# First mixer of a decoder trunk: values of eight heads projected at once as [token, feature], masks and key stacks made by transfers, one pool for weights and values

## The chip, the cores and the metric

The kernel runs on one core of one Trainium2 chip. The metric is the device time of one execution in microseconds (us), as the median of three runs. TensorE is written PE (its weight load PEld), VectorE DVE, ScalarE ACT, GpSimd POOL and SyncE SP. SP here only starts transfers; POOL starts some too.

## The reference, cut to what matters

The computation is a trunk of two layers over 512 positions of 1024 features, in float32. The stage that the change touches is the first mixer, "hybrid", which has eight dilated heads (A) and eight sparse heads (B):

```python
def hybrid_ab_mixer(u, table, w_in, cq_g, wq_b, wq_idx, w_out):
    proj = u @ w_in
    qa, ka, va, cq, kb, vb, k_idx, w_idx = jnp.split(proj, _offsets(EVEN_SIZES), axis=-1)
    o_a = dilated_mixture(qa, ka, va, table[:, :A_HEADS])
    cq = rmsnorm(cq, cq_g)
    qb = cq @ wq_b
    q_idx = cq @ wq_idx
    o_b = dsa_attention(qb, kb, vb, q_idx, k_idx, w_idx, table[:, A_HEADS:], topk)   # topk = 128
    return jnp.concatenate([o_a, o_b], axis=-1) @ w_out

def one_block(...):                      # of dsa_attention, 128 queries at a time
    sc = relu(q_idx . k_idx)             # 8 index heads of 32 features
    score = sum over heads of sc * w_idx
    idx = top_k(where(s <= t, score, -inf), 128)
    logits = q . k[idx] * dh**-0.5 + bias[dist]
    o = softmax(logits) @ v[idx]
```

Around it the first layer has a SwiGLU feed-forward block before and one behind, each added by half; the second layer is the same with a sliding-window mixer in the middle.

## The kernel before, in words

All 512 positions lie in the chip's memory as eight tiles of 128 features x 512 tokens. Every float32 operand is kept as a high and a low part, and a product is three matmuls (L389, L390 and L391 in `chunk`, the helper of the projections; L869 to L871 in `out_proj`). A program, `Plan.emit`, writes down the order of every engine's instructions before the kernel is built: each operation has a cost and a due time, each pool of tiles a number of slots (`CAPACITY`: 58 half tiles "s2", 8 banks "ps", 20 weight tiles "d4", 2 value tiles "v"). The engines then run these orders as written; an instruction that waits holds up all behind it on its engine. The same is true of the transfers started by SP and by POOL.

The stages follow one another: feed-forward, hybrid, feed-forward, feed-forward, sliding, feed-forward. Each stage starts with a norm, whose sums over features are matmuls with a column of ones (L452).

In the hybrid stage `project(j)` makes, for one pair of heads j, three things. Values: a projection as [feature, token], scaled on DVE (`v_turned`, L740), transposed by four PE matmuls with the identity (L744), and split into high and low by ACT (L755) and DVE (L325, the helper of all subtractions). Keys: `k_stack` scales on DVE (L717), and each of two heads gets a tile of 128 partitions that holds its 64 features twice, the high part by ACT (L399) and a copy on ACT (L725) or POOL (L728), the low part by two subtractions (L325) of 64 x 512 on DVE or POOL. Queries: `q_stack` (L701, L399, L325), the subtraction on DVE or POOL. A pair of A heads takes its query weights from `hyb_in`, a pair of B heads from `wq_b`.

`select` makes the masks of the B heads. PE computes the index scores (L964), ACT the relu (L967), DVE the weighted sum (L971 to L978). For the query blocks 1, 2 and 3 DVE then runs sixteen rounds of "eight largest" (L986) and "replace them" (L988), and closes each block (L994) with a bf16 mask that is zero where a key was taken and very negative elsewhere. These steps are strung through the order of DVE between the work of the A heads.

`head` has, for each of four query blocks of 128, 256, 384 and 512 keys: score matmuls (L780, L781), in a B head a further matmul that adds the mask to the bank (L783: the bf16 identity times the mask), a DVE step that adds the position bias and takes the row bound (L787), the exponential on ACT (L796). Then reciprocal (L806), the normalisation on POOL (L813) or ACT (L817), transposes (L829), the split by ACT (L831) and DVE (L325), the product with the values (L845, L846), and the output in ACT (L850) and DVE (L851). `out_proj` follows for all heads in two parts. The bias of a head is one transfer of 256 KB out of a table (`toeplitz`, L693, SP).

A weight tile that "lands" is loaded by SP (L338), split on ACT (L356, L357), and its low part is finished by a transfer started by POOL (L359) that adds the original to the negated high part. In the hybrid stage most weights come like this.

## Time and profile before

| | us |
|---|---|
| three runs | 1829.66, 1831.09, 1831.96 |
| median | 1831.09 |
| the profiled execution, whole | 1832.38 |
| its span on the core | 1830.6 |
| PE busy in the span | 1807.2 |

The profiled execution lies 1.29 us above the median, and 1.78 us of it lie outside the span. The granted clock of PE was 0.995 of full speed over the span. The page gives for each engine the time in which it was executing. The stage views give the same for a stretch. The timelines list single instructions with their start and duration; matmuls overlap their successors, so that the distance between two starts, not the duration, is what one of them takes.

### The profile page before, as it was taken

What the parts mean: (1) busy time and instruction counts of PE and PEld (TensorE: products, weight loads), DVE (VectorE), ACT (ScalarE), POOL (GpSimd) and SP (SyncE); (2) the same over time, 40 slices, a digit from 0 to 9 for tenths busy, and PEclk for the clock granted to TensorE, in tenths of its full rate; (3) what the DMA queues carried; (4) which work ended last, traced back from release to release, by engine and by line L of the source; (5) the groups of instructions that cost most, each with busy time, mean ns of one, the idle gap of its engine ahead of it and who ended that gap; (6) DMA issues with size and microseconds to landing.
All of it is one profiled execution on the core that took longest, in us unless ns stands there. A gap on an engine that the chain in (4) does not pass through costs nothing.

```text
span 1830.6 us, 28269 instructions
## 1 busy us (share of the span) xinstructions
PE 1807.2 (99%) x11036; PEld 1612.7 (88%) x11036; DVE 1319.3 (72%) x2225; ACT 969.2 (53%) x1600; POOL 170.5 (9%) x228
## 2 busy tenths in 40 slices
PE   9999999999999999999999999999999999999997
PEld 6889989888878889998998989989788889899896
DVE  8575857559977897586588866848468798577483
ACT  6343625658768555253355534625679755255263
POOL 2100000115524000000000000000124200000000
PEclk9999999999999999999999999999999999999999
DMA  6713423785745314232343224313844523243231
GB/s 215 245 58 114 122 64 113 198 209 119 162 112 138 103 48 126 92 105 81 109 117 97 83 91 127 118 56 105 229 95 102 150 70 116 70 127 116 70 104 46
DMA packets 75141, 211.55 MB, mean 116 GB/s; under 512 B 12976, under 2 KB 17168, under 8 KB 75008
## 3 DMA queue, kind: packets, MB, share of 16 engines
q1 hardware_dynamic: 58176, 176.88, 30.6%
q0 software_dynamic: 16688, 32.85, 9.8%
q8 instruction: 86, 1.41, 0.3%
q14 instruction: 47, 0.39, 0.1%
q10 hardware_dynamic: 144, 0.03, 0.0%
HBM read 205.92 MB, written 8.47 MB: 117 GB/s over the span
## 4 chain that ended last, share of the span: by engine, by line
PE 89%; DVE 4%; ACT 3%; DMA 2%; issue 1%; POOL 0%; SPq 0%; DVEq 0%; ACTq 0%; POOLq 0%
PE ps L389 14%; PE ps L390 14%; PE ps L391 14%; PE ps L613 12%; PE ps L615 12%; PE ps L614 12%; DVE d L325 1%; PE ps L869 1%; PE ps L870 1%; PE ps L871 1%; PE ps L829 1%; ACT s L796 1%; DMA d<-in_w 1%; PE ps L1155 1%; PE ps L1157 1%
## 5 line engine op out<-in xcount | busy, mean ns | idle before, releaser
L325 DVE TENSOR_TENSOR d<-d,d 128x1024 fp32r<-128x1024 f32 (+3 forms) x415 | 448.8, 1096 | 186.6 <-ACT d L346 138.3
L346 ACT CAST d<-d 128x1024 fp32r<-128x1024 f32 (+3 forms) x415 | 388.0, 949 | 328.6 <-DMA d<-in_w 209.0
L613 PE MATMUL ps<-s,d 128*128 128x256 f32 x1904 | 539.5, 283 | 0.0
L615 PE MATMUL ps<-s,d 128*128 128x256 f32 x1904 | 538.8, 283 | 0.0
L614 PE MATMUL ps<-s,d 128*128 128x256 f32 x1904 | 538.8, 283 | 0.0
L389 PE MATMUL ps<-s,d 128*128 128x512 f32 (+1 forms) x1252 | 496.0, 396 | 2.2 <-DVE d L325 2.0
L390 PE MATMUL ps<-s,d 128*128 128x512 f32 (+1 forms) x1252 | 489.8, 391 | 0.4 <-DVE s L411 0.3
L391 PE MATMUL ps<-s,d 128*128 128x512 f32 (+1 forms) x1252 | 489.2, 391 | 0.0
L613 PEld LDWEIGHTS ps<-s,d 128*128 128x128 f32 x1904 | 365.4, 192 | 0.5
L614 PEld LDWEIGHTS ps<-s,d 128*128 128x128 f32 x1904 | 365.4, 192 | 0.4
L615 PEld LDWEIGHTS ps<-s,d 128*128 128x128 f32 x1904 | 365.4, 192 | 0.0
L391 PEld LDWEIGHTS ps<-s,d 128*128 128x128 f32 (+1 forms) x1252 | 235.8, 188 | 50.2
L389 PEld LDWEIGHTS ps<-s,d 128*128 128x128 f32 (+1 forms) x1252 | 236.2, 189 | 49.7 <-DVE d L325 2.9
L390 PEld LDWEIGHTS ps<-s,d 128*128 128x128 f32 (+1 forms) x1252 | 236.2, 189 | 46.9 <-DVE s L411 1.2
L626 ACT COPY d<-ps 128x512 f32<-128x512 f32 x136 | 79.8, 587 | 250.0 <-PE ps L615 249.7
L685 DVE SCALAR_TENSOR_TENSOR s<-ps,s 128x512 f32<-128x512 f32 x88 | 60.7, 690 | 140.9 <-PE ps L391 140.9
L325 DVE TENSOR_TENSOR s<-s,s 128x512 fp32r<-128x512 f32 (+2 forms) x190 | 126.4, 675 | 8.8 <-ACT s L399 6.4
L565 DVE TENSOR_TENSOR d<-d 128x512 f32<-128x512 f32 x136 | 91.6, 688 | 2.3
L565 DVE TENSOR_TENSOR d<-d,d 128x512 f32<-128x512 f32 x136 | 90.2, 687 | 1.5
L629 DVE TENSOR_TENSOR d<-ps,d 128x512 f32<-128x512 f32 x102 | 70.1, 687 | 16.8 <-PE ps L615 16.1
L359 POOL DMA_DIRECT2D d<-in_swa_in x10 | 8.7, 865 | 731.6 <-DMA d<-in_swa_in 693.2
L356 ACT CAST d<-d 128x1024 fp32r<-128x1024 f32 (+3 forms) x69 | 55.0, 807 | 32.6 <-DMA d<-in_swa_in 13.4
(152 smaller groups left out, 1929.9 us busy)
## 6 DMA issues: line engine op xcount, KB each, us to landing
d<-in_w SPq DMA_DIRECT2D x238, 512.0 KB, 3.7
d<-in_w SPq DMA_DIRECT2D x32, 384.0 KB, 3.1
d<-in_hyb_in SPq DMA_DIRECT2D x22, 512.0 KB, 5.5
d<-in_hyb_in POOLq DMA_DIRECT2D x22, 512.0 KB, 6.7
d<-in_swa_in SPq DMA_DIRECT2D x10, 512.0 KB, 5.5
d<-in_swa_in POOLq DMA_DIRECT2D x10, 512.0 KB, 7.6
tab<-rv POOLq DMA_DIRECT2D x4, 1024.0 KB, 20.0
s<-tab SPq DMA_DIRECT2D x16, 256.0 KB, 5.5
```

Source lines behind the costliest of these rows:

```text
L325: return lambda: eng.tensor_sub(out(), a(), b().bitcast(F32))
L346: alts = [("act", ns[0](n), lambda: nc.scalar.copy(hl.at(0, o), raw.t[:, c]))]
L389: nc.tensor.matmul(o, wl, xh.t, start=i == 0, stop=False)
L390: nc.tensor.matmul(o, wh, xl.t, start=False, stop=False)
L391: nc.tensor.matmul(o, wh, xh.t, start=False, stop=i == n - 1)
L565: return lambda: eng.tensor_add(o.t[:, oc], a.t[:, ac], o.t[:, oc])
L613: nc.tensor.matmul(o, wl, xh, start=start and m == 0 and k == 0, stop=False, skip_group_check=True)
L614: nc.tensor.matmul(o, wh, xl, start=False, stop=False, skip_group_check=True)
L615: nc.tensor.matmul(o, wh, xh, start=False, stop=k == 3, skip_group_check=True)
L626: self.act(act_ns(S, False), lambda: nc.scalar.copy(view(q, c), bank(ps)), [ps], [(q, key)])
L629: self.dve(vec_ns(S), lambda: nc.vector.tensor_add(view(q, c), bank(ps), view(q, c)), [ps, (q, key)], [(q, key)])
L685: self.dve(dve_ns(S), lambda ps=ps, x=x: nc.vector.scalar_tensor_tensor(x.t, ps.t, 0.5, x.t, op0=OP.mult, op1=OP.add), [ps, x], [x])
```

## The change

Only the hybrid stage is rewritten; the sliding stage shares `k_stack`, `v_split` and `head`.

- Values. `values()` is called for j = 0 and j = 4, for four pairs of heads each. The x tiles are now the stationary side, 128 tokens wide, and 512 columns of weights (all eight heads) the moving side; the product lies in four banks "mv" as [token, feature], as the product with the probabilities needs it. There is no scaling by a tile of row factors (L740) and no transpose (L744) in this stage: the row factor is one number per partition, applied by the ACT copy (high part) and a DVE step (low part). The number of matmuls is the same.
- Masks. The mask matmul and the bf16 identity go. For each B head `masked()` starts four transfers of its bias by SP, of 128, 256, 384 and 512 keys, and three by POOL that add the mask of the blocks 1, 2 and 3 to it in place, from the score tile itself, which now holds the mask in float32.
- Key stacks. One ACT copy and one DVE subtraction make the high and low part of both heads in a tile of 128 x 1024, and four transfers by SP, of 64 partitions and 256 KB, copy them into the two stacks.
- Pools. Value tiles and key tiles take slots of the weight pool, which has 22 now.

The diff, cut to its core:

```diff
-CAPACITY = {"s2": SLOTS, "ps": 8, "d4": 20, "v": 2}
+CAPACITY = {"s2": SLOTS, "ps": 8, "d4": 22}
...
+    def masked(self, tab, h, masks):
+        nc = self.nc
+        b, c = Buf("d4", "toepb", (128, 1024)), self.s2("toepc")
+        out = [(c, 384), (c, 0), (b, 512), (b, 0)]
+        for qb, (buf, at) in enumerate(out):
+            n = (qb + 1) * 128
+            key = (buf, at)
+            self.dma(lambda buf=buf, at=at, n=n: nc.sync.dma_start(buf.t[:, at:at + n], tab[h][:, S - n:]),
+                     [("tab", S, h // 4)], [key], n * 512, self.vt - MASKED)
+            if masks[qb] is not None:
+                self.dma(lambda buf=buf, at=at, n=n, m=masks[qb]: nc.gpsimd.dma_start(
+                    buf.t[:, at:at + n], m.t[:, :n], accum_op=OP.add), [masks[qb], key], [key], n * 512,
+                    self.vt - MASKED + 2000, "pool")
+        return out
...
-    def k_stack(self, ps, rows, pool=True):
+    def k_stack(self, ps, rows):
+        f, both = self.s2("tmp"), Buf("d4", "kt", (128, 1024), F32R)
+        self.dve(vec_ns(S), lambda: nc.vector.tensor_mul(f.t, ps.t, rows.t), [ps, rows], [f])
+        hi, lo = Half(both, 0), Half(both, 1)
+        self.hi(hi, f)
+        self.sub(lambda: lo.t, lambda: f.t, lambda: hi.t, [f, hi], [lo], S, ns=vec_ns)
         k = []
         for h in range(2):
-            kh, kl = self.pair("k")
-            self.hi(kh, f, own, (kh, 0))
...
-            for i, out in enumerate((own, oth)):
-                self.sub(lambda kl=kl, out=out: kl.t[out], lambda own=own: f.t[own],
-                         lambda kh=kh, own=own: kh.t[own], [f, (kh, 0)], [(kl, i)], S, pool)
+            for i in range(2):
+                self.dma(lambda b=b, i=i, h=h: nc.sync.dma_start(
+                    b.t[i * 64:i * 64 + 64].bitcast(F32), both.t[h * 64:h * 64 + 64].bitcast(F32)),
+                    [hi, lo], [(kh, i), (kl, i)], 262144)
...
+    def values(self, src, ops, rs):
+        ps = [self.bank("mv") for _ in range(4)]
+        for u in range(4):
+            w = self.unit(src[:, u * 1024:u * 1024 + 1024], 1024, lands=True)
+            for tb in range(4):
+                def f(u=u, tb=tb, w=w):
...
+                        nc.tensor.matmul(ps[tb].t, xh.t[:, c], wl, start=u == 0 and i == 0, stop=False)
+                        nc.tensor.matmul(ps[tb].t, xl.t[:, c], wh, start=False, stop=False)
+                        nc.tensor.matmul(ps[tb].t, xh.t[:, c], wh, start=False, stop=u == 3 and i == 1)
...
+        for tb in range(4):
+            v = Buf("d4", "v", (128, 8, 2, 64), F32R)
+            self.act(sca_ns(S, 1), lambda v=v, src_=src_, r=r: nc.scalar.activation(
+                v.t[:, :, 0], src_(), AF.Copy, scale=r()), [ps[tb], rs], [(v, 0)])
+            self.dve(vec_ns(S) + 50, lambda v=v, src_=src_, r=r: nc.vector.scalar_tensor_tensor(
+                v.t[:, :, 1], src_(), r(), v.t[:, :, 0].bitcast(F32), op0=OP.mult, op1=OP.subtract),
...
-                if m is not None:
-                    nc.tensor.matmul(ps.t[:, :n], self.identb, m.t[:, :n], start=False, stop=True)
...
-            ps = proj(8 + j if j < 4 else 14 + j, pool=pool)
-            V[j] = self.v_split(self.v_turned(ps, R))
-            K[j] = self.k_stack(proj(4 + j if j < 4 else 10 + j, pool=pool), R, pool or True)
+            if j % 4 == 0:
+                V[j] = self.values(t["hyb_v"][j // 4], ops, rs)
+            V[j] = V[j - j % 4]
+            K[j] = self.k_stack(proj(4 + j if j < 4 else 10 + j, pool=pool), R)
             if j < 4:
-                Q[j] = self.q_stack(proj(j, pool=pool), R, pool or True)
+                Q[j] = self.q_stack(proj(j, pool=pool), R)
...
-                masks[qb] = Buf("s2", "mask", (128, S), BF16)
+                masks[qb] = sc
```

What this moves in the order of the engines is shown at two places.

On PE, at the start of the stage, behind the norm's column sums. A row is line, operation, output bank, stationary and moving tile, and shape; d and s are weight and half tiles. Before, the first index score (L964) stands behind the first value projection:

```order
L389 MATMUL ps<-s_3454,d_3339 128x512
L390 MATMUL ps<-s_3464,d_3337 128x512
L391 MATMUL ps<-s_3454,d_3337 128x512
L932 MATMUL ps<-ident,s_3607 128x104 x4
L964 MATMUL ps<-s_3612,s_3626 128x256
L389 MATMUL ps<-s_3224,d_3371 128x512
```

Now, at the end of the first `values()` call:

```order
L784 MATMUL ps<-d_3463,s_3468 128x512
L785 MATMUL ps<-d_3456,s_3479 128x512
L786 MATMUL ps<-d_3456,s_3468 128x512
L1009 MATMUL ps<-s_3620,s_3632 128x256
L1009 MATMUL ps<-s_3620,s_3643 128x256
L389 MATMUL ps<-s_3244,d_3520 128x512
```

All 96 matmuls of `values()` stand ahead of the first index score (L1009 now), where 24 of the first value projection stood.

On DVE, where the last and longest mask is closed (L994 before, L1039 now), with what each instruction waits for in brackets; `m` holds the eight largest, s_3991 (now s_4035) is the score tile of query block 3. Before, the next head's step (L787) reads a bank that PE has added the mask to:

```order
L988 MATCH_REPLACE s_3991<-m_5233,s_3991 128x512 [waits DVE_49]
L994 TENSOR_SCALAR s_5242<-s_3991 128x512 [waits DVE_49]
L740 TENSOR_TENSOR s_5257<-ps,s_3539 128x512 [waits PE_49,Pool_49]
L787 ISA s_5275,stat<-ps,s_4366 128x512 [waits PE_49,Pool_49]
L787 ISA stat 128x1
```

Now the head's step (L830) reads the bias tile d_601 and waits for the transfer that adds the mask to it (DMASW7, started by POOL):

```order
L1039 TENSOR_SCALAR s_4035<-s_4035 128x512 [waits DVE_49]
L717 SCALAR_TENSOR_TENSOR s_5343<-ps,s_3705 128x512 [waits PE_49]
L325 TENSOR_TENSOR d_5341<-s_5334,d_5341 128x512 [waits DMASW6_49,Activation_49]
L325 TENSOR_TENSOR s_5350<-s_5343,s_5350 64x512 [waits Activation_49]
L325 TENSOR_TENSOR s_5356<-s_5343,s_5356 64x512 [waits Activation_49]
L733 TENSOR_TENSOR s_5390<-ps,s_3546 128x512 [waits PE_49]
L717 SCALAR_TENSOR_TENSOR s_5403<-ps,s_3705 128x512 [waits PE_49]
L830 ISA s_5408,stat<-ps,d_601 128x512 [waits DMASW7_49]
```

Six DVE instructions stand between the close and the wait; PE's next score bank comes free only behind that step.

## Rows read from the trace of the kernel before

**Rows 1.** The page, busy time, share of the span and instructions of each engine.
```profile
PE 1807.2 (99%) x11036; PEld 1612.7 (88%) x11036; DVE 1319.3 (72%) x2225; ACT 969.2 (53%) x1600; POOL 170.5 (9%) x228
```

**Rows 2.** Busy time by stretch: PE, PEld, DVE, ACT, POOL, clock, DMA share, GB/s.
```profile
440.00:500.00 60.00, 60.00 (x317) 50.81 (x317) 58.33 (x176) 47.30 (x107) 36.40 (x45) 1.00 0.67 150
500.00:560.00 60.00, 55.50 (x290) 44.39 (x290) 45.96 (x102) 40.37 (x90) 23.30 (x31) 1.00 0.54 113
367.00:640.00 273.00, 266.59 (x1360) 219.43 (x1359) 224.54 (x550) 195.16 (x399) 94.03 (x113) 1.00 0.58 140
```

**Rows 3.** Line L452 in the hybrid stage: durations, first and last start.
```profile
L452 PE MATMUL ps<-ones,s x24: 164/250/271, 367.1 to 630.5; 128*128 128x1 f32 x24
```

**Rows 4.** PE's waits, 367 to 640 us: waited for, total, times, longest.
```profile
PE ps L845 <- DVE d L325: 1.9, 4, 0.8
PE ps L829 <- ACT s L817: 1.4, 1, 1.4
```

**Rows 5.** PE timeline, block 3 of the first B head: start, duration, instruction.
```profile
522.83 0.39 PE L781 MATMUL ps<-d,s 128*128 128x512 f32 x1
523.06 0.39 PE L783 MATMUL ps<-s,identb 128*128 128x512 bf16 x1
...
523.46 0.45 PE L389 MATMUL ps<-s,d 128*128 128x512 f32 x1
```

**Rows 6.** PE timeline at one group of value transposes.
```profile
416.89 0.60 PE L744 MATMUL ps<-ident,s 128*128 128x128 f32 x4
417.25 0.48 PE L389 MATMUL ps<-s,d 128*128 128x512 f32 x1
417.56 0.39 PE L390 MATMUL ps<-s,d 128*128 128x512 f32 x1
```

**Rows 7.** DVE in 367 to 640 us by line and shape: count, busy, mean ns.
```profile
L325 DVE TENSOR_TENSOR d<-s,d 64x512 fp32r<-64x512 f32 x15 | 15.4, 1027 | 2.0 <-ACT d L399 1.8
...
L325 DVE TENSOR_TENSOR s<-s,s 64x512 fp32r<-64x512 f32 x8 | 5.5, 685 | 2.2 <-ACT s L399 2.1
L740 DVE TENSOR_TENSOR s<-ps,s 128x512 f32<-128x512 f32 x8 | 5.5, 684 | 3.2 <-PE ps L391 3.2
```

**Rows 8.** DVE timeline, the first weighted index score.
```profile
391.44 0.28 DVE L971 TENSOR_SCALAR s<-s,wts 128x128 f32<-128x128 f32 x1 [0.23 <-ACT s L967]
```

**Rows 9.** DVE timeline, the close of the last mask and the next head.
```profile
522.21 0.43 DVE L994 TENSOR_SCALAR s<-s 128x512 bf16<-128x512 f32 x1
522.55 0.69 DVE L740 TENSOR_TENSOR s<-ps,s 128x512 f32<-128x512 f32 x1
```

**Rows 10.** Transfers started by POOL (L359), 500 to 560 us: issue ns, landing.
```profile
L359 POOL DMA_DIRECT2D d<-in_hyb_out x7: 822/856/879, 523.1 to 557.1; - x7
...
DMA to landing us min/median/max: 3.5/6.3/9.7
```

**Rows 11.** ACT timeline in the A heads.
```profile
469.57 0.61 ACT L796 ACTIVATE s<-s,stat 128x384 f32<-128x384 f32 x1
...
470.17 0.60 ACT L817 ACTIVATE s<-s,stat 128x384 f32<-128x384 f32 x1
470.68 0.71 ACT L796 ACTIVATE s<-s,stat 128x512 f32<-128x512 f32 x1
...
471.39 0.56 ACT L755 CAST v<-ps 128x512 fp32r<-128x512 f32 x1
471.86 1.05 ACT L356 CAST d<-d 128x1024 fp32r<-128x1024 f32 x1
```

**Rows 12.** DMA of 367 to 640 us: packets and MB; an issue's KB, us to landing.
```profile
DMA packets 15256, 38.11 MB, mean 140 GB/s; under 512 B 1962, under 2 KB 2986, under 8 KB 15235
...
s<-tab SPq DMA_DIRECT2D x12, 256.0 KB, 4.6
```

**Rows 13.** DVE timeline, one key subtraction beside one on POOL.
```profile
399.40 1.83 DVE L325 TENSOR_TENSOR d<-s,d 64x512 fp32r<-64x512 f32 x1
```

**Rows 14.** POOL timeline at the same moment.
```profile
399.39 1.30 POOL L325 TENSOR_TENSOR d<-s,d 64x512 fp32r<-64x512 f32 x1 [0.66 <-ACT d L399]
```

More of the change, by code (lines that the diff above doesn't have):

```diff
@@ L757, in v_split, with src_, head @@
         return v
-    def head(self, q, k, tt, v, vi, o, half, masks=None, band=None):
+    def values(self, src, ops, rs):
+        nc = self.nc
+        ps = [self.bank("mv") for _ in range(4)]
[3 more added lines that the diff above has]
+                def f(u=u, tb=tb, w=w):
+                    c = slice(tb * 128, tb * 128 + 128)
+                    for i in range(2):
+                        (xh, xl), at = ops[2 * u + i], slice(i * 512, i * 512 + 512)
+                        wh, wl = w.at(0, at), w.at(1, at)
+                        nc.tensor.matmul(ps[tb].t, xh.t[:, c], wl, start=u == 0 and i == 0, stop=False)
+                        nc.tensor.matmul(ps[tb].t, xl.t[:, c], wh, start=False, stop=False)
+                        nc.tensor.matmul(ps[tb].t, xh.t[:, c], wh, start=False, stop=u == 3 and i == 1)
+                self.pe(6 * pe_ns(S), f, self.parts(w) + [x for xs in ops[2 * u:2 * u + 2] for x in xs], [ps[tb]])
+        out = []
+        for tb in range(4):
+            v = Buf("d4", "v", (128, 8, 2, 64), F32R)
+            def src_(tb=tb):
+                return ps[tb].t.rearrange("p (h d) -> p h d", d=64)
+            r = lambda tb=tb: rs.t[:, tb:tb + 1]
+            self.act(sca_ns(S, 1), lambda v=v, src_=src_, r=r: nc.scalar.activation(
+                v.t[:, :, 0], src_(), AF.Copy, scale=r()), [ps[tb], rs], [(v, 0)])
+            self.dve(vec_ns(S) + 50, lambda v=v, src_=src_, r=r: nc.vector.scalar_tensor_tensor(
+                v.t[:, :, 1], src_(), r(), v.t[:, :, 0].bitcast(F32), op0=OP.mult, op1=OP.subtract),
+                [ps[tb], rs, (v, 0)], [(v, 1)])
+            out.append(v)
+        return out
+    def head(self, q, k, tt, v, vi, o, half, band=None):
         nc = self.nc
@@ L774, in head, with f, g @@
             ps = self.bank("sc")
-            m = masks[qb] if masks is not None else None
+            tb, tc = tt[qb] if isinstance(tt, list) else (tt, t0)
+            tk = (tb, tc) if isinstance(tt, list) else tt
             pi, pc = place[qb]
-            def f(qb=qb, ps=ps, s0=s0, n=n, m=m):
+            def f(qb=qb, ps=ps, s0=s0, n=n):
                 qs = q.t[:, qb * 128:(qb + 1) * 128]
                 nc.tensor.matmul(ps.t[:, :n], qs, kl.t[:, s0:s0 + n], start=True, stop=False)
-                nc.tensor.matmul(ps.t[:, :n], qs, kh.t[:, s0:s0 + n], start=False, stop=m is None)
-                if m is not None:
-                    nc.tensor.matmul(ps.t[:, :n], self.identb, m.t[:, :n], start=False, stop=True)
-            self.pe((2 if m is None else 3) * pe_ns(n), f, kr + ([m] if m is not None else []), [ps])
-            def g(qb=qb, ps=ps, n=n, t0=t0, c=(pi, pc)):
+                nc.tensor.matmul(ps.t[:, :n], qs, kh.t[:, s0:s0 + n], start=False, stop=True)
+            self.pe(2 * pe_ns(n), f, kr, [ps])
+            def g(qb=qb, ps=ps, n=n, tb=tb, tc=tc, c=(pi, pc)):
                 nc.vector.tensor_tensor_reduce(
-                    out=prob[c[0]].t[:, c[1]:c[1] + n], in0=ps.t[:, :n], in1=tt.t[:, t0:t0 + n], scale=1.0,
+                    out=prob[c[0]].t[:, c[1]:c[1] + n], in0=ps.t[:, :n], in1=tb.t[:, tc:tc + n], scale=1.0,
                     scalar=3.0e38 if band is None else self.sinkn[:, band:band + 1],
                     op0=OP.add, op1=OP.min, accum_out=st.t[:, qb:qb + 1])
-            self.dve(dve_ns(n), g, [ps, tt] + (["sink"] if band is not None else []),
+            self.dve(dve_ns(n), g, [ps, tk] + (["sink"] if band is not None else []),
                      [(prob[pi], qb), (st, 0, qb)])
@@ L1014, in attend @@
             for i in range(2):
-                self.head(Q[j][i], K[j][i], T.pop(0), V[j], i, o[j], i, masks if j >= 4 else None)
+                self.head(Q[j][i], K[j][i], T.pop(0), V[j], 2 * (j % 4) + i, o[j], i)
                 if T_next:
-                    T.append(self.toeplitz(self.tab0, T_next.pop(0), S))
+                    h = T_next.pop(0)
+                    T.append(self.toeplitz(self.tab0, h, S) if h < 8 else self.masked(self.tab0, h, masks))
         o = []
@@ L1273 @@
 LANDS = 6000.0
+MASKED = 10000.0
+LAT = 4000.0
 ROOM = 1200.0
```

41 lines of the change are left out of this document (18 added, 23 removed).

## The prediction

> **What bounds the kernel now.** I read the page first: PE is busy 1807.2 us of the 1830.6 us span, 99%, and DVE 72%, ACT 53% [rows 1]. So the kernel ends when PE has done its matmuls, and an edit pays by taking matmuls away or by filling PE's gaps. The busy time by stretch says where gaps are: in 367 to 640 us, which holds the hybrid stage, PE is busy 266.59 of 273 us, so it is idle 6.41, and 4.5 of these lie in 500 to 560, where the last mask is closed and the first B heads start [rows 2]. The list of PE's waits names DVE's and ACT's split of the probabilities for half of it [rows 4]. The stage itself runs from the first to the last column sum, 367.1 to 630.5: 263.4 us [rows 3]. All below is against that number, in us from 367.1. Inside it DVE is nearly a second bound: 58.33 of 60 us in 440 to 500 [rows 2]. That is the selection: from the first weighted score at 391.44 [rows 8] to the close of the last mask at 522.21 [rows 9] there are 130.8 us in which DVE runs 48 rounds and the work of the A heads in between. PE's order is laid out around this chain.
>
> **What leaves PE.** The mask matmul takes the distance of two starts, 523.06 less 522.83, 0.23 us for 512 columns; the 0.63 us from L781 to the next L389 hold it, L781's own 0.23 and the two small matmuls of the next block, which leaves 0.2 to 0.26 [rows 5]. A head has it with 256, 384 and 512 columns; in proportion that is 0.12 + 0.17 + 0.23 = 0.52, and eight heads make 4.2. A group of four value transposes takes 417.25 less 416.89 = 0.36, and the matmul behind it 0.31 instead of 0.23, 0.08 more [rows 6]; eight groups make 2.9 to 3.5. Nothing takes their place on PE: `values()` has as many 512-column matmuls as the four projections had, only with the sides exchanged. The floor falls by 7.1 to 7.7; I take **7.3**. With PE's gaps as they are, the stage would end at 256.1.
>
> **What moves the selection.** Before, 24 value matmuls stand ahead of the first index score, now all 96. The 72 more cost 72 x 0.23 = 16.6 us, so the first weighted score comes at about 24.3 + 16.6, less 1 for small work that came earlier: 40. DVE's rows from there to the last close come to as much as before by their counts and durations. In the whole stage DVE loses 8 scalings of 0.684 and 15 key subtractions of 1.027 on 64 partitions, and gains 8 subtractions of about 0.68 and six query subtractions of 0.685 that POOL had [rows 7]: 20.9 out, 9.5 in. But the saving is used up in that stretch by work of the A heads and of the values that the later start brings into it. So I keep 130.8, and the last mask closes at 171, not at 155.1 (522.21 less 367.1). It is behind that close that this change adds its wait: POOL issues the mask's addition (0.86 us) and it lands in 3.5 to 9.7, median 6.3, by the row of the same kind of transfer with weights [rows 10]. No row shows it with both ends in the chip; I take 6.3 and keep the ends for the range. **The masks can be used at 178.2** (175 to 182). DVE has six instructions of 0.68 = 4.1 us to do in the meantime, then it waits some 3 us; PE's next bank waits for it. By the count of matmuls, PE arrives there after 732 pitches of 512 columns. In the old order 632 pitches ended at 155.7 (522.83 less 367.1) [rows 5], so 732 end at about 178 to 180 when scaled, less if gaps close. The wait is nearly covered, because three key and query projections were pulled ahead of it.
>
> **What follows the masks.** Before, the B heads had 630.5 less 522.21 = 108 us behind the close. Now they have 256.1 less 171 = 85 if all the 7.3 are to be kept, and the eight heads stand close together. There ACT is the tight one. Start to start, its exponential of 384 columns with its read takes 0.60, of 512 columns 0.71, a normalisation of 384 columns 0.51, a split of 512 columns 0.47 [rows 11]. A B head has four exponentials (0.38 + 0.49 + 0.60 + 0.71, the first two by the same step of 0.11), splits of 1.22, a copy of 0.47 and two normalisations: 4.8. The order has 7.25 heads of this behind the masks: 35. With 20 weight casts of 0.5, 6 of 0.95 and 8 small ones of 0.5 it is 54.5. Behind the last head's values PE has 99 matmuls of 0.23, 22.8, and the eight column sums, 1. The stage then ends at 178.2 + 54.5 + 23.8 = **256.5** if ACT never waits. It will: ACT stood idle 20 of the 60 us in 500 to 560 [rows 2]. I add 2.8 for the first head's start and for late masks, nearest to the 4.5 that PE lost there before: 259.3. That is 4.1 less than 263.4; the profiled run would give 1832.38 less 4.1 = 1828.3, the median 1831.09 less 4.1 = **1827.0**.
>
> **Keys and POOL.** On POOL the change takes away 17 key and six query subtractions and nine copies, and puts 24 issues of 0.86 = 21 us in their place. A key subtraction on DVE took 1.83 us at 399.40, while POOL ran its own of 1.30 from 399.39 [rows 13, 14], against 0.685 for the query kind [rows 7]; I price the new ones at 0.68. The Trainium skill, page "SBUF — State Buffer", section "Who interferes with whom", says that a DVE instruction with two SBUF inputs and a GpSimd instruction that reads SBUF exclude each other. Those two rows agree; by this rule POOL's normalisations, which stay, would still lengthen the 22 new ones, and at 1.03 instead of 0.68 the sum would be up to 7.7 us more on DVE, of which only those before the last close, about half, would reach the end, 3.9: 1831 at the most. The stack itself now comes by four transfers behind the DVE step; the nearest row lands in 4.6 us [rows 12], where copies and subtractions took about as long. It is hidden as long as the projections run ahead, three pairs of them at the masks; without that cover it is some 5 us for each pair. The sliding stage builds one stack the same way, at 0 to +3; I take 0. The other stages keep their instructions.
>
> **Rivals.** *The full gain or more* (0.22): landing is quick, DVE's saving shortens the chain, and PE finds work at each step. Then the stage has the old gaps, 256.1 and 1823.8, or loses half of the 6.4 too: 1820.6. For it: POOL's slow steps are gone; against: ACT's 54.5. *No change* (0.22): ACT's and DVE's in-order rows behind the late masks cost 4 us more than I added, so that the 7.3 are lost as gaps of PE: 1829.5 to 1834.8, middle 1831. For it speaks that the selection starts 16 us later and nothing shortens it. *Slower, by the transfers* (0.21): from the close to the last B head SP starts 12 stack copies of 256 KB, five biases of 640 KB and seven weights, 8.2 MB, and POOL 17 mask additions and two weights, 4.1 MB. The stage moved 140 GB/s at a DMA share of 0.58 [rows 2], so 241 at a share of one (an estimate); the 12.3 MB take 51 us at that rate, and about 45 to 51 are there. If additions inside the chip run below it, at 200, it is 61, the masks of heads 11 to 15 come 10 us late, PE has no other matmuls left, and the stage ends at 269: 1836.7. POOL holds it up too, since normalisations stand behind additions that wait for their bias. It decides from the point where an addition lands later than about 10 us after its issue. The Trainium skill, page "DMA: Bandwidth & Descriptors", section "Issuing engines are not separate DMA queues", says that transfers of all issuing engines end up on the same 16 DMA engines and interleave. It speaks against this change: by it the additions of POOL and the copies of SP slow each other, which is this rival and its 1836.7; the trace of before has no such crowd.
>
> **How the numbers follow.** My forecast, 1827.0, has 0.35 with the times from 1824.5 to 1829.5. Faster or slower by 0.2%, 3.7 us, is about what a measurement of this kernel can tell from no change, so that the bounds are 1827.4 and 1834.8, and the first cuts this case: 0.22 of it is faster, 0.13 within. With the full gain, 0.22, faster has 0.44; with the case of no change, 0.22, within has 0.35; slower has 0.21. The range leaves out a tenth on either side: down to the full gain with half the gaps, 1820, up to the late masks, 1839.
>
> **What would show it.** PE's matmul time of the stage falls by 7 us. The first L1009 starts at 39 to 40 us after the first L452 and the close of the last mask (L1039) at 169 to 174. PE's largest gap lies just behind it, in matmuls that wait for DVE L830, and DVE's for the addition L702. ACT is above nine tenths from there for 50 us. Stage: 259 us. It is wrong if the masks close as early as before, if additions land in over 10 us, or if PE waits for key stacks (L742).

## The result: slower by 1%, and the profile after

The changed kernel took 1850.52 us (median of four runs, 1848.64 to 1852.81) against 1831.53 beside it: a ratio of 1.0103, 95% interval 1.0087 to 1.0119. I had forecast 1827.0 and a range up to 1839. The profiled execution took 1849.39 us, its span 1847.6, 17.0 more than before.

The page's first part for the kernel after, to be set against [rows 1]: PE has 56 instructions fewer, as it should, and is busy as long as before.

```profile
PE 1807.5 (98%) x10980; PEld 1612.5 (87%) x10980; DVE 1307.7 (71%) x2210; ACT 960.2 (52%) x1591; POOL 150.1 (8%) x213
```

The column sums (L452) open each stage. Their first starts give the stages' lengths: feed-forward, hybrid, feed-forward, feed-forward, sliding, feed-forward. Two of these lines, of the kernel after, the start of the first block and that of the hybrid stage:

```profile
L452 PE MATMUL ps<-ones,s x8: 164/250/250, 19.2 to 19.9; 128*128 128x1 f32 x8
...
L452 PE MATMUL ps<-ones,s x8: 250/250/271, 378.4 to 379.2; 128*128 128x1 f32 x8
```

and of the kernel before the start of the first block (the hybrid stage's is [rows 3]):

```profile
L452 PE MATMUL ps<-ones,s x8: 164/250/250, 20.0 to 20.7; 128*128 128x1 f32 x8
```

| stage, first L452 to first L452, us | before | after | difference |
|---|---|---|---|
| up to the first | 20.0 | 19.2 | -0.8 |
| feed-forward 1 | 347.1 | 359.2 | +12.1 |
| hybrid | 262.6 | 273.3 | +10.7 |
| feed-forward 2 | 346.3 | 346.5 | +0.2 |
| feed-forward 3 | 350.2 | 346.2 | -4.0 |
| sliding | 146.8 | 143.8 | -3.0 |
| last, with the end | 357.6 | 359.4 | +1.8 |

So there are two losses, and one of them lies in a stage that the diff does not name. Busy time of the two stretches in the kernel after (PE, PEld, DVE, ACT, POOL, granted clock, DMA share, GB/s):

```profile
19.20:378.40 359.20, 351.92 (x2090) 312.55 (x2089) 236.00 (x329) 160.60 (x220) 17.19 (x20) 0.99 0.44 132
378.40:652.50 274.10, 256.36 (x1259) 212.29 (x1259) 206.67 (x516) 186.51 (x387) 74.91 (x99) 0.97 0.83 192
```

and of the kernel before, the first block and then the hybrid stage on the same bounds, 367.1 to 630.5:

```profile
20.00:367.10 347.10, 347.10 (x2087) 310.43 (x2086) 236.47 (x329) 159.92 (x218) 17.16 (x20) 1.00 0.44 133
...
367.10:630.50 263.40, 256.99 (x1316) 211.46 (x1315) 217.68 (x529) 191.37 (x392) 94.03 (x113) 1.00 0.59 139
```

The hybrid stage's sum closes on these rows. PE is idle 274.10 - 256.36 = 17.74 us, before 6.41: 11.3 more. Its busy time should have fallen by the 7.3 us of matmuls taken out, to 249.7; it is 256.36, so what is left took 6.7 us longer. The granted clock says why: a mean of 0.97 of full speed where it was 1.00. 11.3 + 6.7 - 7.3 = 10.7. The 6.7 is what is left over when 7.3 is taken for the matmuls that went. A count that doesn't use the 7.3 comes near it: in the stage PE was busy for about 15 us at the lower of its two clock levels (0.50 of full speed, at 541 to 544, 565 to 571 and 592 to 599 us), which costs half of that, 7.5 us, and leaves 8.1 us that went. In the first block the same split is 7.3 idle (5.3 of it at 105 to 112 us, the rest at 375 to 378, just ahead of the hybrid stage) and 4.8 more busy time, 12.1.

### The profile page after: what moved, and what is told of

Read it like the earlier page. It is cut to its first block, busy times and chain, and to the rows that moved or that the text cites. A ratio compares the mean times of both kernels' runs of the same rounds, so it can differ in the third digit from the quotient of the medians.

```text
span 1847.6 us, 28262 instructions
## 1 busy us (share of the span) xinstructions
PE 1807.5 (98%) x10980; PEld 1612.5 (87%) x10980; DVE 1307.7 (71%) x2210; ACT 960.2 (52%) x1591; POOL 150.1 (8%) x213
## 4 chain that ended last, share of the span: by engine, by line
PE 87%; DVE 5%; DMA 3%; ACT 2%; issue 1%; SPq 0%; POOL 0%; DVEq 0%; ACTq 0%; POOLq 0%
PE ps L390 13%; PE ps L389 13%; PE ps L391 13%; PE ps L613 12%; PE ps L615 12%; PE ps L614 12%; DVE d L325 1%; PE ps L872 1%; PE ps L913 1%; PE ps L914 1%; PE ps L915 1%; DMA d<-d 1%; DVE s L325 1%; ACT s L839 1%; PE ps L784 1%
## 5 line engine op out<-in xcount | busy, mean ns | idle before, releaser
L346 ACT CAST d<-d 128x1024 fp32r<-128x1024 f32 (+3 forms) x415 | 385.4, 948 | 397.2 <-DMA d<-in_w 181.1
L389 PE MATMUL ps<-s,d 128*128 128x512 f32 (+1 forms) x1188 | 469.9, 396 | 8.0 <-ACT s L399 4.6
L390 PE MATMUL ps<-s,d 128*128 128x512 f32 (+1 forms) x1188 | 467.3, 393 | 2.7 <-DVE s L411 2.0
L391 PE MATMUL ps<-s,d 128*128 128x512 f32 (+1 forms) x1188 | 465.8, 392 | 0.0
L389 PEld LDWEIGHTS ps<-s,d 128*128 128x128 f32 (+1 forms) x1188 | 224.9, 189 | 55.7 <-ACT s L399 5.1
L390 PEld LDWEIGHTS ps<-s,d 128*128 128x128 f32 (+1 forms) x1188 | 225.0, 189 | 49.3 <-DVE s L411 4.6
L391 PEld LDWEIGHTS ps<-s,d 128*128 128x128 f32 (+1 forms) x1188 | 224.8, 189 | 47.6
L356 ACT CAST d<-d 128x512 fp32r<-128x512 f32 (+3 forms) x69 | 55.1, 806 | 32.0 <-DMA d<-in_hyb_in 15.0
L839 ACT ACTIVATE s<-s,stat 128x256 f32<-128x256 f32 (+3 forms) x128 | 65.9, 516 | 8.7 <-DVE stat L830 8.4
```

The costliest lines, as they stand in the source:

```text
L346: alts = [("act", ns[0](n), lambda: nc.scalar.copy(hl.at(0, o), raw.t[:, c]))]
L389: nc.tensor.matmul(o, wl, xh.t, start=i == 0, stop=False)
L390: nc.tensor.matmul(o, wh, xl.t, start=False, stop=False)
L391: nc.tensor.matmul(o, wh, xh.t, start=False, stop=i == n - 1)
L839: nc.scalar.activation(x, x, AF.Exp, bias=st.t[:, qb:qb + 1], scale=-1.0, accum_out=st.t[:, 4 + qb:5 + qb])
```

## The first block: twelve bias loads that nobody had asked for so early

SP's timeline in the kernel after. A row may hold several transfers (the count is at its end):

```profile
42.76 2.01 SPq L338 DMA_DIRECT2D d<-in_w  x2
60.86 0.33 SPq L699 DMA_DIRECT2D s<-tab  x1
61.29 0.37 SPq L699 DMA_DIRECT2D d<-tab  x1
...
68.55 0.32 SPq L699 DMA_DIRECT2D d<-tab  x1
70.23 4.79 SPq L338 DMA_DIRECT2D d<-in_w  x4
```

These are the bias tiles of the first three B heads, which are not needed before 540 us. SP stands before them until the table is built, then starts twelve loads, and the weights of the feed-forward block come behind. From 44 to 70 us SP started one weight load, in the kernel before six. Five microseconds at a time, after:

```profile
65.00:70.00 5.00, 5.00 (x24) 4.14 (x23) 0.00 (x0) 0.00 (x0) 0.56 (x1) 1.00 0.97 275
70.00:75.00 5.00, 5.00 (x23) 4.14 (x23) 0.00 (x0) 0.00 (x0) 0.00 (x0) 1.00 1.06 357
...
105.00:110.00 5.00, 0.57 (x3) 0.15 (x1) 5.00 (x12) 3.79 (x8) 0.00 (x0) 1.00 0.27 110
110.00:115.00 5.00, 4.08 (x9) 3.00 (x10) 5.00 (x11) 2.19 (x5) 0.00 (x0) 0.58 0.00 0
115.00:120.00 5.00, 5.00 (x18) 3.99 (x17) 4.72 (x6) 2.87 (x5) 0.00 (x0) 0.74 0.38 108
```

DVE and ACT, which split each weight tile, have next to nothing to do from 65 to 80 us. What they didn't do then falls on 100 to 120, where DVE has the block's other work as well and is full; PE waits 4.64 us for it, and its granted clock is 0.58 and 0.74 on the mean of the two stretches of five microseconds behind the gap. The wait itself, on PE (in brackets the idle time before and what ended it):

```profile
110.22 0.50 PE L389 MATMUL ps<-s,d 128*128 128x512 f32 x1 [4.64 <-ACT s L399]
```

The old bias tiles could not be taken so early: the table `AHEAD` holds them back to 30 us before they are due. The new kinds are not in it. **e1_bias_late** puts them in (a line of three dots in an edit, here and below, stands for lines left out):

```diff
-AHEAD = {'toep': 30000.0, 'sx': 8000.0}
+AHEAD = {'toep': 30000.0, 'toepb': 30000.0, 'toepc': 30000.0, 'sx': 8000.0}
```

> The kernel after, with one line changed: the bias tiles of the B heads may be taken at most 30 us ahead of their due time, as the bias tiles of the A heads already are, so that SP starts them in the hybrid stage and not at 61 to 69 us in the first feed-forward block. Theory 1 (two losses, both by transfers: bias loads ahead of the first block's weights, 12 us, and crowded transfers in the hybrid stage, 11 us): the first block falls from 359.2 to 347 or 348 us, the hybrid stage stays at 270 to 276, the whole near 1839. Rival (the stall at 105 us comes from the new order of the first block as such): the first block stays at 355 or more, the whole near 1850.

The block fell to 347.4 us, the hybrid stage stayed (275.0), as theory 1 had it. The whole, 1844.51 (1838.74 to 1846.04), ratio 1.0082 (1.0065 to 1.0098), is 6 below the kernel after by the medians, and 5.5 above what was expected; the profiled execution, 1838.74, is the fastest of the four and 10.7 below. So the block's 12 us are shown by the trace, but not all of them in every run's total. Was it the loads or the three weight tiles that the early bias held? **e6_19_slots** takes three away from the start:

```diff
-CAPACITY = {"s2": SLOTS, "ps": 8, "d4": 22}
+CAPACITY = {"s2": SLOTS, "ps": 8, "d4": 19}
```

> As e1_bias_late with 19 instead of 22 weight tiles, the number that the kernel after had in its first block while three bias tiles were held there. It tells what cost 11.8 us in the first feed-forward block. If the twelve bias loads ahead of the weights in SP's order did it, the block stays at 347 to 350 us; if the three missing tiles did it, it takes 355 or more. The hybrid stage may lose by the missing tiles, which is not the question here.

The block took 348.5 us: 19 tiles are enough for it, and it was the loads in SP's order. The hybrid stage seems to need the tiles: it took 282.6 and the whole 1861.12, in a single run.

## The hybrid stage: which part costs

PE's waits in the stage of the kernel after, to be set against [rows 4]: for what, total, times, longest.

```profile
PE ps L825 <- DMA d<-d: 6.0, 2, 5.5
PE ps L872 <- POOL s L856: 4.5, 1, 4.5
PE ps L825 <- DVE s L1033: 3.8, 1, 3.8
```

The first is the scores of a head waiting for its key stack (L742), the second the transposes waiting for POOL's normalisation, the third a bank that DVE holds before the close. All three lie behind 530 us. Two theories stood against each other: the crowd of transfers (theory 1), and the selection that starts later (rival 2). Four kernels undo or keep single parts; each, like e1, gets a new order from the kernel's own planner, which is the weakness of this set.

**e2_no_ktransfer** has the old key stacks (with e1's line):

```diff
-                self.dma(lambda b=b, i=i, h=h: nc.sync.dma_start(
-                    b.t[i * 64:i * 64 + 64].bitcast(F32), both.t[h * 64:h * 64 + 64].bitcast(F32)),
...
+            self.p.op([("act", act_ns(S), dup_act), ("pool", pool_ns(S), dup_pool)], [f], [(kh, 1)], self.vt)
+            for i, out in enumerate((own, oth)):
+                self.sub(lambda kl=kl, out=out: kl.t[out], lambda own=own: f.t[own],
...
```

> As e1_bias_late, and the key stacks are made on ACT, DVE and POOL again as in the kernel before (the query subtractions may go to POOL again too); values and masks stay as changed. It takes 32 transfers of 256 KB, 8 MB, out of the hybrid stage. Theory 1 (the crowd of transfers is what costs): DMA share behind the masks falls from about 1.0 to 0.8, PE's wait of 6.0 us for key transfers goes, the stage comes to 262 to 268 us, the whole to 1829 to 1835. Rival 2 (the selection that starts 16 us later costs, whatever carries keys and masks): the stage stays at 270 or more, the whole at 1838 or more.

**e3_mask_matmul** has the old masks:

```diff
-                nc.tensor.matmul(ps.t[:, :n], qs, kh.t[:, s0:s0 + n], start=False, stop=True)
+                nc.tensor.matmul(ps.t[:, :n], qs, kh.t[:, s0:s0 + n], start=False, stop=m is None)
+                if m is not None:
+                    nc.tensor.matmul(ps.t[:, :n], self.identb, m.t[:, :n], start=False, stop=True)
...
```

> The kernel after with the masks added by the 24 matmuls again and one bias transfer for each head; values and key transfers stay as changed. No bias is loaded in the first block, so that this is to be set beside e1_bias_late. It takes 24 additions by POOL (4.6 MB) and 3 MB of bias out and puts 4.2 us of matmuls in. Theory 1: the close is followed by PE at once, the waits for DVE and POOL behind it (3.8 and 4.5 us) go, the clock falls less: stage 262 to 268, whole 1829 to 1835. Rival 2: 270 or more, 1838 or more.

**e4_values_only** has both of these old parts.

> The kernel before with the values part alone: values for eight heads at once as [token, feature], tiles in the weight pool of 22; masks by matmul and key stacks on the engines as before. PE has 3.2 us less than before, and the index scores still stand behind 96 matmuls. Theory 1: stage 259 to 264 us, whole 1827 to 1833. Rival 2 (the later selection costs): stage 268 or more, whole 1836 or more.

**e8_no_values** has the old values with e1's masks and keys:

```diff
-            if j % 4 == 0:
-                V[j] = self.values(t["hyb_v"][j // 4], ops, rs)
-            V[j] = V[j - j % 4]
+            ps = proj(8 + j if j < 4 else 14 + j, pool=pool)
+            V[j] = self.v_split(self.v_turned(ps, R))
...
```

> As e1_bias_late without the values part: masks and keys by transfers, values by projection and transposes as before, so that the first index score stands behind 24 value matmuls again. PE has 4.2 us less than in the kernel before. Theory 1 (masks and keys together crowd the transfers, whatever the values do): the stage is still long, 268 us or more, whole 1836 or more. Rival 3 (the later selection squeezes the B heads and their transfers into too short a time, and only that makes the crowd): stage 256 to 263, whole 1823 to 1830.

All kernels but e6 in one table (v, m and k are the change's values, masks and keys, half k half of the key transfers). MB, DMA share, stage and PE's idle time are of the profiled execution's hybrid stage, first to last L452; median and ratio are of all runs against those of the kernel before beside them (median 1830.2, for the kernel after 1831.5).

| kernel | values, masks, keys by the change | MB | DMA share | stage us | PE idle | median us | ratio (95%) |
|---|---|---|---|---|---|---|---|
| before | - - - | 36.5 | 0.59 | 263.4 | 6.4 | | 1 |
| after | v m k | 52.5 | 0.83 | 274.1 | 17.7 | 1850.52 | 1.0103 (1.0087 to 1.0119) |
| e1 | v m k | 52.6 | 0.81 | 275.0 | 17.9 | 1844.51 | 1.0082 (1.0065 to 1.0098) |
| e2 | v m - | 44.0 | 0.71 | 260.8 | 8.0 | 1827.61 | 0.9986 (0.9977 to 0.9996) |
| e3 | v - k | 44.9 | 0.73 | 256.8 | 3.9 | 1823.96 | 0.9967 (0.9956 to 0.9979) |
| e4 | v - - | 35.4 | 0.56 | 261.8 | 5.7 | 1821.75 | 0.9964 (0.9948 to 0.9979) |
| e8 | - m k | 52.1 | 0.79 | 277.3 | 21.1 | 1843.66 | 1.0080 (1.0065 to 1.0095) |
| e5 | v - k, unread masks | 54.2 | 0.80 | 283.7 | 21.2 | 1850.95 | 1.0118 (1.0101 to 1.0135) |
| e7 | v m half k | 48.1 | 0.76 | 270.2 | 15.7 | 1833.48 | 1.0027 (1.0015 to 1.0038) |
| e9 | v - half k | 40.4 | 0.66 | 256.1 | 2.5 | 1818.99 | 0.9941 (0.9923 to 0.9959) |
| e10 | v - k, unread biases | 50.2 | 0.75 | 267.5 | 11.7 | 1833.13 | 1.0020 (1.0010 to 1.0030) |
| e11 | v - k, unread copies | 48.8 | 0.73 | 272.3 | 13.0 | 1834.41 | 1.0029 (1.0015 to 1.0043) |
| e12 | e11, small copies | 44.9 | 0.71 | 263.3 | 9.1 | 1829.11 | 0.9999 (0.9987 to 1.0011) |
| e13 | e1, small additions | 48.1 | 0.77 | 265.1 | 12.8 | 1827.68 | 0.9995 (0.9985 to 1.0005) |

Rival 2 falls. In e3 and e4 the index scores stand behind 96 value matmuls as in the kernel after, the last mask closes 169.6 and 169.5 us after the stage's start, and both are faster than before. In e8 they stand behind 24 again, and the stage is as long as ever. So it is not the values: alone they gain 8.4 us. Little of that is the stage's own, which is 1.6 shorter in e4's profiled execution; feed-forward 3 and the sliding stage are 7.0 shorter. With the keys by transfer the gain is 6.2, which the intervals don't part from the 8.4, with the masks 2.6, though the masks take another 4.2 us of matmuls off PE; with both it is a loss of 14.3. Theory 1 had the direction of all three right and their times too long: e2 came out 1.4 us below its range, e3 and e4 5 below theirs. What keys and masks share is the transfers.

## The hybrid stage: crowd, chain or queue

Transfers can cost in two ways: by holding up other transfers (theory 1a), or because a head now waits for a chain of close, addition, landing (1b). **e5_crowd** is e3 with all transfers of `masked()` beside it, into tiles that nothing reads:

```diff
                     T.append(self.toeplitz(self.tab0, h, S))
+                    if h >= 8:
+                        self.masked(self.tab0, h, source)
```

> As e3_mask_matmul (values and key transfers changed, masks added by matmuls), and beside it every bias load of `masked()` and every addition by POOL into the same kind of tiles, which nothing reads. So the transfers, their slots and POOL's issues are those of e1_bias_late (plus the old bias loads, 2 MB), but no head waits for a mask that was added by a transfer. Theory 1a (the crowd: transfers lengthen each other and hold up key transfers and weights): stage 266 us or more, PE waits for key transfers, whole 1833 or more. Theory 1b (the chain: close, POOL's addition, landing, DVE step, PE bank, and the order laid out for it): stage 257 to 261, whole 1823 to 1828.

The stage went from e3's 256.8 to 283.7. No head waits for an added mask there: the transfers, with their tiles, their issues and the order laid out for them, do it without that chain. **e10_bias_only** and **e11_mask_only** take the crowd apart:

```diff
-            if masks[qb] is not None:
-                self.dma(lambda buf=buf, at=at, n=n, m=masks[qb]: nc.gpsimd.dma_start(
-                    buf.t[:, at:at + n], m.t[:, :n], accum_op=OP.add), [masks[qb], key], [key], n * 512,
-                    self.vt - MASKED + 2000, "pool")
```

> As e5_crowd without the 24 additions by POOL: the bias loads of `masked()` remain, 32 transfers by SP of 64 to 256 KB, 5.2 MB in all, into tiles that nothing reads. It takes e5_crowd's load apart. If the bytes that SP moves between the key transfers cost (queue of SP, memory reads), the stage is 268 us or more, whole 1834 or more. If the additions are needed for the loss, the stage is 257 to 262, whole 1823 to 1829.

```diff
-            self.dma(lambda buf=buf, at=at, n=n: nc.sync.dma_start(buf.t[:, at:at + n], tab[h][:, S - n:]),
-                     [("tab", S, h // 4)], [key], n * 512, self.vt - MASKED)
...
-                    buf.t[:, at:at + n], m.t[:, :n], accum_op=OP.add), [masks[qb], key], [key], n * 512,
+                    buf.t[:, at:at + n], m.t[:, :n]), [masks[qb]], [key], n * 512,
```

> As e5_crowd without the bias loads: 24 transfers by POOL of the same mask tiles with the same sizes, 4.6 MB, as plain copies into tiles that nothing reads, so that POOL never waits for a bias. If the bytes inside the chip and POOL's 24 issues cost by themselves, the stage is 268 us or more, whole 1834 or more. If it takes bias loads and additions together (POOL's queue standing still for a bias that is late), the stage is 257 to 262, whole 1823 to 1829.

Neither is free: 267.5, just short of its first case (as is the whole, 1833.13), and 272.3 (e11's profiled execution, 1840.73, lies 6 above its median, so its stage is too long by some of that). By the medians they cost 9 and 10 us against e3; both together 27. In e10 the wait that comes up is the key stacks: PE waits 8.1 us for them, in e3 1.4. These waits lie at 449 to 496 us, ahead of the last close: the crowd comes earlier there. Before the longest, 5.3 us, the key transfers took 7.5 to 8.9 us to land, at a DMA share of 1.06 from 456 to 468 us. In e11 the longest wait is another, 5.0 us for a subtraction on DVE; for key stacks PE waits 2.8.

Three explanations of that are left: bytes, the number of issues and landings, or the new order. **e12_small_copies** and **e13_small_adds** answer with every engine's order unchanged and only the size cut:

```diff
-                    buf.t[:, at:at + n], m.t[:, :n]), [masks[qb]], [key], n * 512,
+                    buf.t[:, at:at + 32], m.t[:, :32]), [masks[qb]], [key], n * 512,
```

> As e11_mask_only, order of every engine unchanged, but each of POOL's 24 unread copies moves 32 columns (16 KB) instead of 256 to 512: 0.4 MB instead of 4.6. It parts bytes from number. If the bytes on the DMA engines cost, the stage falls from 272 to 258 to 264 us and the whole to 1823 to 1829. If the 24 issues and their landings in POOL's and the transfers' queues cost, whatever their size, or the order that was laid out around them, the stage stays at 268 or more, the whole at 1832 or more.

```diff
-                    buf.t[:, at:at + n], m.t[:, :n], accum_op=OP.add), [masks[qb], key], [key], n * 512,
+                    buf.t[:, at:at + 32], m.t[:, :32], accum_op=OP.add), [masks[qb], key], [key], n * 512,
```

> As e1_bias_late, order of every engine unchanged, but each of the 24 mask additions covers 32 columns (16 KB) only: the rest of the mask is left out of the output. The bias loads, the waits and the key transfers stay. If the additions' bytes cost, the stage falls from 275 to 262 to 269 us and the whole from 1844 to 1831 to 1838. If their number, the waits for bias tiles and the order cost, it stays at 272 or more, the whole at 1840 or more.

e13 is the plainest result of the study. 24 additions of fewer bytes, 4.5 MB less of 52.6, nothing else, and the stage falls from 275.0 to 265.1, the median from 1844.51 to 1827.68, a little below what I had written down. e12 falls from 1834.41 to 1829.11, at the upper end of its first case. The bytes cost. Of the stage's 9.9 us, 5.1 are PE's idle time and 4.8 its busy time, at a granted clock of 0.97 in e1 and 0.99 in e13. The waits that shrink are those for key stacks (L825) and for POOL's normalisations (L872), in e1 and then in e13:

```profile
PE ps L825 <- DMA d<-d: 6.4, 4, 2.5
PE ps L872 <- POOL s L856: 4.5, 4, 2.1
```

```profile
PE ps L872 <- POOL s L856: 1.7, 3, 1.2
PE ps L825 <- DMA d<-d: 1.7, 2, 1.3
```

Stretches behind the close in e1 and then in e13 (PE, PEld, DVE, ACT, POOL, clock, DMA share, GB/s):

```profile
541.00:561.00 20.00, 16.61 (x80) 13.19 (x78) 10.51 (x30) 11.27 (x27) 7.40 (x11) 1.00 1.08 247
561.00:581.00 20.00, 15.05 (x80) 11.79 (x81) 13.53 (x35) 14.28 (x38) 10.98 (x15) 0.93 1.10 242
581.00:601.00 20.00, 20.00 (x107) 17.44 (x106) 14.49 (x42) 16.60 (x44) 9.72 (x14) 0.90 1.05 266
```

```profile
541.00:561.00 20.00, 17.50 (x91) 13.86 (x90) 12.50 (x36) 12.36 (x32) 8.74 (x14) 1.00 1.11 239
561.00:581.00 20.00, 17.80 (x98) 14.38 (x97) 14.43 (x39) 16.16 (x41) 12.77 (x16) 1.00 0.99 234
581.00:601.00 20.00, 19.24 (x109) 16.02 (x108) 14.32 (x40) 19.88 (x51) 9.38 (x15) 1.00 0.73 185
```

In e1 the DMA engines are full for all sixty microseconds, at 242 to 266 GB/s; in e13 for some forty. While they are full transfers land later. In the kernel after a key transfer lands in 3.1 to 11.9 us, median 7.0, a mask addition in 2.6 to 12.5, median 7.6 (the old additions took 6.3 [rows 10], the old bias loads 4.6 [rows 12]):

```profile
DMA to landing us min/median/max: 3.1/7.0/11.9
```

```profile
DMA to landing us min/median/max: 2.6/7.6/12.5
```

The key transfers of this kernel again, first those ahead of the last close and then those of the sixty microseconds behind it:

```profile
DMA to landing us min/median/max: 3.1/5.1/9.2
```

```profile
DMA to landing us min/median/max: 6.7/9.7/11.9
```

SP in the kernel after. The four transfers of one pair's stacks (L742) go out in the first row; the next ones stand between bias loads (L699):

```profile
551.91 5.79 SPq L742 DMA_DIRECT2D d<-d  x4
...
561.96 1.91 SPq L699 DMA_DIRECT2D s<-tab  x1
563.97 0.47 SPq L742 DMA_DIRECT2D d<-d  x1
564.49 0.58 SPq L699 DMA_DIRECT2D d<-tab  x1
```

These four landed 7.4 to 11.9 us after their issue, and PE gets the head's keys at 565.87, 5.46 us late:

```profile
565.87 0.45 PE L825 MATMUL ps<-d,s 128*128 128x128 f32 x1 [5.46 <-DMA d<-d]
```

From there on the in-order queues pass it on. POOL a little later: an addition waits 9.38 us for its bias, and a normalisation (L856) that is ready stands behind it:

```profile
569.52 0.87 POOL L702 DMA_DIRECT2D d<-s  x1 [9.38 <-DMA d<-tab]
570.48 0.58 POOL L856 TENSOR_SCALAR s<-s,stat 128x384 f32<-128x384 f32 x1
```

The same happens before 591.94, where an addition has waited 4.73 us, and PE's transposes wait for the normalisation behind it (timeline of PE):

```profile
592.79 1.24 PE L872 MATMUL ps<-ident,s 128*128 128x128 f32 x3 [4.55 <-POOL s L856]
```

Behind each of these two gaps PE runs at less than its full clock. The stretches that hold these two gaps in the kernel after:

```profile
560.00:570.00 10.00, 4.54 (x14) 3.49 (x13) 3.04 (x10) 5.58 (x15) 0.61 (x2) 0.74 1.07 227
590.00:600.00 10.00, 7.14 (x27) 6.06 (x28) 3.86 (x10) 4.19 (x11) 5.45 (x7) 0.66 1.11 291
```

**e7_half_k** shows the dose from the other side: e1 with half the key bytes, the own half written by ACT and DVE:

```diff
-        f, both = self.s2("tmp"), Buf("d4", "kt", (128, 1024), F32R)
...
+            self.hi(kh, f, own, (kh, 0))
+            self.sub(lambda kl=kl, own=own: kl.t[own], lambda own=own: f.t[own],
+                     lambda kh=kh, own=own: kh.t[own], [f, (kh, 0)], [(kl, 0)], S, ns=vec_ns)
+            self.dma(lambda b=b, own=own, oth=oth: nc.sync.dma_start(
+                b.t[oth].bitcast(F32), b.t[own].bitcast(F32)),
...
```

> As e1_bias_late (values, masks and keys changed), but each head's own 64 partitions of the key stack are written by ACT and DVE directly and only the other 64 are copied: 16 key transfers of 256 KB instead of 32, 4 MB less, for 8 more steps of 64 x 512 on ACT and on DVE. Theory 1a (crowd): about half of the way from e1_bias_late's 275.0 us to e2_no_ktransfer's 260.8: stage 264 to 270, whole 1830 to 1838. Theory 1b (chain): the stage stays at 272 or more, since the mask's chain is the same.

270.2, at the upper edge of the range and about a third of the way to e2 (by the medians, 1833.48, two thirds). The wait for key stacks is gone from its list; the wait for POOL's normalisations, 5.9 us, is not.

What bytes don't settle: e13 and e7 move the same 48.1 MB, and their stages are 265.1 and 270.2, so the kind and the place of the bytes count too. e13 keeps 12.8 us of gaps, against e3's 3.9, at a full DMA in part of the stage; how much of the rest is the order's and how much the 3 MB of bias wasn't tried.

**e9_half_k_matmul** leaves out what costs and keeps what pays: values at once, masks by matmul, half the key transfers (e3 with e7's edit).

> As e3_mask_matmul (values and keys changed, masks added by matmuls) with only the foreign 64 partitions of each key stack copied: 16 key transfers of 256 KB instead of 32. Theory 1 (the crowd is what costs; without mask transfers it is below the bound): at or a little below e3_mask_matmul, stage 255 to 259 us, whole 1820 to 1825. If eight more steps on ACT and DVE weigh more than 4 MB of transfers, the stage is 260 to 262, as in e4_values_only, whole 1825 to 1828.

1818.99 us (1818.12 to 1821.14), ratio 0.9941 (0.9923 to 0.9959): faster than both kernels. Its stage and PE's longest waits in it:

```profile
368.10:624.20 256.10, 253.62 (x1278) 208.38 (x1282) 211.56 (x522) 184.74 (x381) 65.19 (x87) 1.00 0.66 158
```

```profile
PE ps L916 <- POOL s L325: 1.5, 1, 1.5
PE ps L452 <- DVE s L427: 0.5, 1, 0.5
```

Of its 14.2 us between the profiled executions (1832.38 and 1818.19), 7.3 are the hybrid stage's. The rest is that of feed-forward 3 and the sliding stage, which are 7.0 shorter here as they are in the kernel after and in nearly all the others: the kernel before waits 3.57 us at the norm ahead of the sliding stage, with a clock of 0.78 around it, and these don't. That stretch of the kernel before:

```profile
1320.00:1330.00 10.00, 6.43 (x25) 5.27 (x24) 2.98 (x12) 5.14 (x6) 1.49 (x2) 0.78 0.89 210
```

Which part of the change removed that wait was not isolated; it has to be one that e4 has, the values or the joint pool. The pool is the likelier: in e6's single run, with 19 tiles, feed-forward 3 took 349.5 and the sliding stage 151.4, and the gain is gone.

## Why the prediction was wrong, by its own steps

For the profiled execution the working gave 1828.3; it took 1849.39, 21.1 more. Of that the first block is 12.1, the hybrid stage 14.8 (274.1 for 259.3), and the other stages, forecast as unchanged, gave 5.8 back.

**What bounds the kernel now.** One reading was off there: half of PE's wait was put to the split of the probabilities on DVE and ACT, but L817 in [rows 4] is the normalisation. Nothing else used it.

**What leaves PE** was right in kind: 24 mask matmuls and 32 transposes went. Its size is borne out roughly: the count by the clock gives 8.1 for the 7.3.

**What moves the selection** was right. The first index score started at 417.2 - 378.4 = 38.8 us (forecast 39 to 40), the last close at 549.9 - 378.4 = 171.5 (171):

```profile
417.24 0.40 PE L1009 MATMUL ps<-s,s 96*128 96x256 f32 x2
```

```profile
549.92 0.42 DVE L1039 TENSOR_SCALAR s<-s 128x512 f32<-128x512 f32 x1
```

The wait behind it was small, as said: DVE lost 0.3 us in all to mask additions. PE's largest gap was not there, as the signs had it, but ended 16 us on, at a key stack. The later close cost nothing that e3 and e4 didn't win back, so that the rival "no change", which rested on it, had the wrong cause.

**"The other stages keep their instructions"** is the first step that failed: 12.1 us by the trace, 6.0 by the medians of the kernel after and e1. PE's, DVE's and ACT's do; SP's don't. The order of SP shows twelve L699 rows in the first block. I had read that queue only around the masks.

**What follows the masks** is the second, and the dearest. I let ACT set the pace, 54.5 us of work, and added 2.8 for late masks: 88 us from the close to the stage's end. It took 102.6 (274.1 - 171.5), with the DMA engines full for most of it. From 550 to 600 us ACT was busy nine tenths in one stretch of ten microseconds, 580 to 590; else it waited with the others. The right course stood among the rivals, slower by the transfers, with 0.21 and 1836.7 us. Its rate was well estimated, 241 GB/s at a full share against 242 to 266 in e1, and so was its place. Its dose was short: e1's sixty microseconds behind the close moved 15.1 MB, where I had counted 12.3 and allowed 45 to 51 us; six more weight loads start in them than I had counted. At 241 GB/s 15.1 MB take 63 us. The rival came to its 61 us by a lower rate, 200 GB/s, than e1 shows, and it had neither the first block nor the clock. Copies by POOL that nothing reads make SP's key transfers late: behind the last close those landed in a median of 10.1 us in e11, and of 7.4 in e12, where the same copies are small. The Trainium skill, page "DMA: Bandwidth & Descriptors", section "Issuing engines are not separate DMA queues", which the rival cited, says that transfers started by different engines interleave on the same 16 DMA engines; e11 and e12 agree.

**No term for the clock** is the third. I priced gaps of PE at their length. In the stage 11.3 us of further gaps brought 6.7 us of longer busy time with them, in the first block 7.3 brought 4.8: here a gap cost about 1.6 times its length. Of the first block's 4.8 some 3 are the clock's (by PE's timeline 6.2 us of busy time at the lower level, half of it lost); the rest was not traced.

**Keys and POOL.** The 128-wide key subtractions took 0.793 us, the query ones 0.686, against 0.68 assumed: less than 1 us, and the 7.7 us of that paragraph weren't needed. The key stack, which I took as hidden by three pairs of projections, was the largest wait (6.0). Two of the signs of being wrong came: additions landed in up to 12.5 us, and PE waited for key stacks.

## What to carry to other kernels

Work moved from an engine to transfers is paid in DMA time of the stretch where it lands: sum the megabytes of that stretch, of all queues, over the share-of-one rate read from the trace, and compare with the time that is left there, before counting what the engine saves. Read that rate from a stretch with the same mixture: at 70 to 75 us, with the table's own transfers and weight loads, it was 357 GB/s at a share of 1.06, behind the close 242 to 266. Read every queue of the new order from its first row, not only at the place of the edit: a new kind of tile that a planner's limits don't name can be loaded hundreds of microseconds early, ahead of what is needed. Where a change has several parts that load the same resource, try each alone and in pairs: here the values alone gained 8 us, with the masks 3 and with the keys 6 (not clearly less than 8), and all three lost 14.

## What the runs showed of the hardware

Twenty-four transfers inside the chip, which add one tile to another, cost 9.9 us of the stage and about 17 us by the medians when they moved 128 to 256 KB each instead of 16 (e1 against e13), in a stage whose DMA share was 0.81 on the mean; the mean hid sixty microseconds at 1.05 to 1.10. And behind a single gap of 4.64 us PE's granted clock went from its upper level, 2.4 GHz, to its lower, 1.2 GHz: on the mean 0.58 of full speed in the first five microseconds and 0.74 in the next, with matmuls that start 0.43 us apart instead of 0.23, and 1.00 from 120 us on.
